# Sequence mixer of a two-layer block: five halving levels and a block of four, a solve without masked copies, the gate product ahead of the core steps

## The chip, the core and the metric

One core of one Trainium2 chip. The metric is the device time of one execution in microseconds (us). The kernel before takes 1794.52 us, the median of 3 runs (1789.35 to 1795.16). TensorE (PE) multiplies matrices, VectorE (DVE) and ScalarE (ACT) work on elements, GpSimd (POOL) here fills and copies a little, and SyncE (SP) issues the loads.

## The reference

256 tokens of width 1024 pass two layers, each a gated feed-forward, a hybrid mixer and a second feed-forward, and then a second block with retention and dilated attention. The change concerns the mixers alone:

```python
proj = h @ w_in            # split into hg_q, hg_f, hg_i, hg_g, gd_q, gd_k, gd_v, gd_z, gd_b, gd_a, rg_x, rg_gate
f = lbf + (1 - lbf) * sigmoid(hg_f)
o_hg = hgrn2_chunked(silu(hg_q) * 64**-0.5, 1 - f, hg_i, log(f))     # forgetting attention
o_hg = head_rmsnorm(o_hg) * silu(hg_g)
qkv = silu(causal_depthwise_conv(concat(gd_q, gd_k, gd_v)))
o_gd = gated_delta_chunked(l2norm(cq) * 128**-0.5, l2norm(ck), cv, g, beta)   # a triangular solve per chunk
o_gd = head_rmsnorm(o_gd) * silu(gd_z)
o_rg = rg_lru(...) * gelu(rg_gate)
return concat(o_hg, o_gd, o_rg) @ w_out
```

The forgetting attention scores a query at t and a key at s by the sum over channels of q k exp(cum_t - cum_s), where cum is the running sum of log f. The delta rule solves (I + L) u = rhs with L strictly lower triangular.

## The kernel before, in words

All wide matmuls are fp32 products in three passes over a high and a low half of each operand. A chunk of weights (128x1024) is loaded, cast on ScalarE to its high half wh (L92) and subtracted on VectorE to its low half wl (L93), in one of three buffers. TensorE then runs the passes, with 256 columns (L184 to L186) or up to 512 (L140 to L142), into one of four PSUM accumulators called mm.

A mixer's steps are written in the order of MIX_ORDER (L490). A scheduler places the recorded instructions on the engines by estimated times, and each engine then runs its own list in order. So small work of one step stands between the wide matmuls of others. The steps that matter here are these, for 256 tokens as two halves of 128.

- `delta_k` makes the matrices LT (line L676 writes them, scr in the trace) for the two halves and the cross part.
- `delta_solve` (twice per mixer) inverts I + L for four heads at once. It masks LT into a 32-block diagonal LTb (L715), a 32-off-diagonal LT32 (L720) and a 64-off-diagonal part (L721), on VectorE, with the sign changed. Then it doubles the block size: per size 2, 4, 8, 16 two groups of four small matmuls (L711, into the PSUM tile sv; x8 in the trace), a masked copy (L728), a transpose (L731) and a copy on ScalarE (L732). The sizes 32 and 64 follow with copies (L739, L750, L756) and scalings (L745, L746) on VectorE and copies and scalings on ScalarE (L743, L749, L759). Each group waits for the elements of the one before.
- `hg_scores` builds the scores S of the forgetting attention in seven halving levels (b = 64 to 1). A level takes differences to a reference position (L901, L902), an exponential on ScalarE, products with k and q (L904, L910), four matmuls and a masked copy into S (L917). The diagonal (t = s) is one product of q and k (L873), four small matmuls (hd, L878; x8 in the trace) and a masked copy of the identity.
- `gates` spreads the decay over 128 columns (gb, L601) before a matmul; `hg_vg` scales the values (L857).
- `delta_core` (twice) makes the delta rule's outputs (Zp, LZ, og). The z projection follows it in MIX_ORDER: 260 columns by `gemm_tok`, then `z_gate`, a tanh on ScalarE (L572) and a product on VectorE (L573). `delta_out` multiplies output, norm and gate (L792) and transposes the result (yT), and `project` runs 96 matmuls of 512 columns with w_out, first for the channels of the other two branches.

## Time and profile before

| | before |
|---|---|
| median of 3 runs | 1794.52 us |
| the profiled execution | 1796.44 us, its span 1794.7 us |
| granted TensorE clock, mean | 0.981 |
| mixer 0, mixer 1 | about 205 to 388 us, 765 to 945 us of the span |
| busy, TensorE, VectorE, ScalarE | 1734.5, 1207.1, 892.3 us |
| share of TensorE in the chain that ended last | 90% |

A wait in brackets behind an instruction is idle time of its engine just before it, with the instruction that ended it. PEclk is the clock granted to TensorE as a share of 2.4 GHz, 0.5 being 1.2 GHz. Only in the mixers, of all of the kernel, does the change alter a line.

### The profile page before, as it was taken

To read this page: it belongs to the slowest core of one execution; us is meant where nothing else is said; L and a number is where in the kernel's file an instruction comes from. 1 tells how busy PE (TensorE), PEld (TensorE's weight loads), DVE (VectorE), ACT (ScalarE), POOL (GpSimd) and SP (SyncE) were. 2 spreads that over 40 slices of the span, in tenths; PEclk is the share of its full clock that TensorE was granted. 3 is DMA by queue.
4 is the path that set the end of the run, shared out by engine and by line. 5 is a ranking of instruction groups with operands and counts; after the bars stand their busy time and mean duration, and the time that the engine had idled before them with its cause. 6 is when DMAs were issued, how large, how long until landed. Compare 5 with 4: busy or idle time off the path is not lost.

```text
span 1794.7 us, 28677 instructions
## 1 busy us (share of the span) xinstructions
PE 1734.5 (97%) x11296; PEld 1568.8 (87%) x11296; DVE 1207.1 (67%) x2181; ACT 892.3 (50%) x1352; POOL 13.4 (1%) x40
## 2 busy tenths in 40 slices
PE   8999989989999999989889999999999999999996
PEld 8997989879998999889879998888888788799885
DVE  6666689866655665589967665745666666766566
ACT  5444574444444444466345444555454544455454
POOL 0000000000000000000000000000000000000000
PEclk9999999899999999999989999999999999999998
DMA  6546542235565555543315556555443456645561
GB/s 233 186 153 220 163 135 84 94 104 185 176 197 189 183 188 181 186 151 118 127 47 177 187 169 199 185 176 173 133 130 124 146 176 211 200 155 198 194 229 53
DMA packets 91654, 292.38 MB, mean 163 GB/s; under 512 B 11008, under 2 KB 23808, under 8 KB 91520
## 3 DMA queue, kind: packets, MB, share of 16 engines
q1 hardware_dynamic: 91376, 290.45, 49.4%
q8 instruction: 88, 1.44, 0.3%
q14 instruction: 46, 0.38, 0.1%
q10 hardware_dynamic: 144, 0.11, 0.0%
HBM read 289.47 MB, written 1.05 MB: 162 GB/s over the span
## 4 chain that ended last, share of the span: by engine, by line
PE 90%; DVE 6%; ACT 2%; issue 1%; DMA 1%; SPq 0%; DVEq 0%; ACTq 0%
PE mm L185 13%; PE mm L186 13%; PE mm L184 13%; PE mm L140 13%; PE mm L141 13%; PE mm L142 13%; PE sv L711 2%; DVE wl L93 1%; ACT wh L92 1%; PE pv L1234 1%; PE dS L658 1%; PE dsc L1202 1%; PE hS L915 1%; PE dsc L1201 0%; DVE cv L630 0%
## 5 line engine op out<-in xcount | busy, mean ns | idle before, releaser
L93 DVE TENSOR_TENSOR wl<-raw,wh 128x1024 fp32r<-128x1024 f32 (+2 forms) x544 | 639.8, 1177 | 462.8 <-ACT wh L92 461.4
L92 ACT CAST wh<-raw 128x1024 fp32r<-128x1024 f32 (+2 forms) x544 | 549.3, 1011 | 652.1 <-PE mm L185 281.0
L184 PE MATMUL mm<-xTh,wh 128*128 128x256 f32 x2112 | 595.6, 284 | 13.1 <-DVE xp L622 10.0
L185 PE MATMUL mm<-xTl,wh 128*128 128x256 f32 x2112 | 598.0, 284 | 2.2 <-DVE xTl L197 2.1
L186 PE MATMUL mm<-xTh,wl 128*128 128x256 f32 x2112 | 595.2, 283 | 0.8 <-DVE wl L93 0.7
L184 PEld LDWEIGHTS mm<-xTh,wh 128*128 128x128 f32 x2112 | 401.4, 191 | 17.9 <-ACT th L572 10.4
L185 PEld LDWEIGHTS mm<-xTl,wh 128*128 128x128 f32 x2112 | 402.5, 191 | 4.7 <-DVE xTl L197 3.7
L186 PEld LDWEIGHTS mm<-xTh,wl 128*128 128x128 f32 x2112 | 403.0, 191 | 2.8 <-DVE wl L93 1.3
L141 PE MATMUL mm<-wl,hT 128*128 128x512 f32 x608 | 241.4, 398 | 2.4 <-DVE wl L93 2.4
L142 PE MATMUL mm<-wh,hT 128*128 128x512 f32 x608 | 238.8, 394 | 0.0
L140 PE MATMUL mm<-wh,hT 128*128 128x512 f32 x608 | 219.3, 397 | 4.8 <-DVE scr L573 4.8
L141 PE MATMUL mm<-wl,xTh 128*128 128x512 f32 (+1 forms) x440 | 169.3, 386 | 0.0
L142 PE MATMUL mm<-wh,xTl 128*128 128x512 f32 (+1 forms) x440 | 166.2, 380 | 0.0
L140 PE MATMUL mm<-wh,xTh 128*128 128x512 f32 (+1 forms) x440 | 160.2, 384 | 2.5 <-ACT xTh L196 2.5
L140 PEld LDWEIGHTS mm<-wh,hT 128*128 128x128 f32 x608 | 114.9, 190 | 30.2 <-DVE scr L573 5.2
L141 PEld LDWEIGHTS mm<-wl,hT 128*128 128x128 f32 x608 | 115.4, 190 | 28.3 <-DVE wl L93 3.9
L142 PEld LDWEIGHTS mm<-wh,hT 128*128 128x128 f32 x608 | 115.2, 189 | 24.7 <-DVE hT L197 0.2
L140 PEld LDWEIGHTS mm<-wh,xTh 128*128 128x128 f32 x440 | 82.0, 188 | 19.0 <-ACT xTh L196 2.9
L142 PEld LDWEIGHTS mm<-wh,xTl 128*128 128x128 f32 x440 | 83.0, 189 | 16.6 <-issue 2.0
L141 PEld LDWEIGHTS mm<-wl,xTh 128*128 128x128 f32 x440 | 82.9, 188 | 16.2 <-issue 1.9
L196 ACT ACTIVATE xTh<-xtr,colp 128x256 fp32r<-128x256 f32 (+1 forms) x72 | 28.9, 453 | 12.4 <-DVE xTl L197 12.3
L711 PE MATMUL sv<-hS,LTm 128*128 128x32 f32 x192 | 27.5, 293 | 7.3 <-ACT hS L732 4.3
...
## 6 DMA issues: line engine op xcount, KB each, us to landing
...
```

The source lines that it names most:

```text
L92: nc.scalar.copy(h, raw)
L93: nc.vector.tensor_tensor(l, raw, h.bitcast(F32), op=ALU.subtract)
L140: nc.tensor.matmul(o, xh[:, kt, tok], wh[:, k], start=a and k == 0, stop=False)
L141: nc.tensor.matmul(o, xh[:, kt, tok], wl[:, k], start=False, stop=False)
L142: nc.tensor.matmul(o, xl[:, kt, tok], wh[:, k], start=False, stop=z and k == m - 1)
L184: nc.tensor.matmul(o, wh[:, k, cs], xh[:, kt], start=a, stop=False)
L185: nc.tensor.matmul(o, wh[:, k, cs], xl[:, kt], start=False, stop=False)
L186: nc.tensor.matmul(o, wl[:, k, cs], xh[:, kt], start=False, stop=z)
L196: nc.scalar.activation(h, src, AF.Copy, scale=scale)
L658: nc.tensor.matmul(ps[:, h], k[:, h, sb * P:(sb + 1) * P], src[:, h, tb * P:(tb + 1) * P], start=True, stop=True)
L711: nc.tensor.matmul(o[:, h], lhsT[:, h], rhs[:, h], start=True, stop=True)
L915: nc.tensor.matmul(ps[:, i], B[:, j, t * P:(t + 1) * P], Q[:, i].rearrange("p h t -> p (h t)"), start=True, stop=True)
```

## The change

`hg_scores` stops halving at b = 4. What is left within blocks of four tokens (on and below the diagonal) is done at once: with differences to the second token of each block, one exponential for q and one of the opposite sign for k, two products, eight matmuls of half the rows, and two masked copies with the constant g4. The diagonal step (hd) goes. Within a level the key product covers only the even halves and is written in place. For b = 64 and 32 the scores go into S by plain copies on ScalarE in place of a masked copy.

`delta_solve` no longer masks. POOL fills LTb and LT32 with zeros and ScalarE copies the blocks into them with the sign changed; the product for size 64 uses the first 64 rows alone. Copies and scalings of the sizes 32 and 64 go from VectorE to ScalarE.

`gates` hands the matmul a broadcast view in place of gb. `hg_vg` scales the values on ScalarE. `delta_out` multiplies output and gate first, then the norm, 512 columns at a time. In MIX_ORDER z stands before the cores.

```diff
-LEVELS = (64, 32, 16, 8, 4, 2, 1)
+LEVELS = (64, 32, 16, 8, 4)
...
+    out["g4"] = ((t // 4 == s // 4) & (t >= s)).T * 1.0
...
-MIX_ORDER = "... dv1 q dv0 dq core0 core1 z dout out".split()
+MIX_ORDER = "... dv1 q dv0 dq z core0 core1 dout out".split()
...
-            gb = v2(c.w2("gb")[:, :4 * P], 4)
-            nc.vector.tensor_copy(gb, bc(g[:, t].unsqueeze(2), [P, 4, P]))
...
-                nc.tensor.matmul(ps[:, h], gb[:, h], c.K["triu"], start=True, stop=True)
+                nc.tensor.matmul(ps[:, h], bc(g[:, t, h:h + 1], [P, P]), c.K["triu"], start=True, stop=True)
...
+        def neg(o, i):
+            nc.scalar.activation(o, i, AF.Copy, scale=-1.0)
...
-        nc.vector.tensor_tensor(LTb, LT, h4(K["bd"]), op=ALU.mult)
+        nc.gpsimd.memset(LTb, 0.0)
+        nc.gpsimd.memset(LT32, 0.0)
+        for q in range(4):
+            neg(LTb[qd(q), :, qd(q)], LT[qd(q), :, qd(q)])
...
-        nc.vector.tensor_tensor(LT32, LT, h4(K["mt32"]), op=ALU.mult)
-        nc.vector.tensor_tensor(LT, LT, h4(K["mt64"]), op=ALU.mult)
+        for q in (0, 2):
+            neg(LT32[qd(q), :, qd(q + 1)], LT[qd(q), :, qd(q + 1)])
...
-            nc.vector.tensor_copy(PF[qd(q), :, qd(q - 1)], ps[qd(q)])
+            nc.scalar.copy(PF[qd(q), :, qd(q - 1)], ps[qd(q)])
...
-            nc.vector.tensor_scalar(T64[:, :, qd(q)], Tc, K["q2"][:, q:q + 1], None, op0=ALU.mult)
-            nc.vector.tensor_scalar(TT64[:, :, qd(q)], TTc, K["q2"][:, q:q + 1], None, op0=ALU.mult)
+            nc.scalar.activation(T64[:, :, qd(q)], Tc, AF.Copy, scale=K["q2"][:, q:q + 1])
+            nc.scalar.activation(TT64[:, :, qd(q)], TTc, AF.Copy, scale=K["q2"][:, q:q + 1])
...
-        nc.vector.tensor_copy(TT64[qd(2), :, 32:64], pq[qd(2)])
+        nc.scalar.copy(TT64[qd(2), :, 32:64], pq[qd(2)])
...
-        mm4(ps, LT, T64)
+        mm4(ps, LT[0:64], T64[0:64])
...
-        nc.vector.tensor_copy(PF[64:, :, 0:64], ps[64:])
+        neg(PF[64:, :, 0:64], ps[64:])
...
-            for h in range(4):
-                nc.vector.scalar_tensor_tensor(yt[:, h], self.og[t][:, h], self.gs[t][:, h:h + 1], sz[:, h],
-                                               op0=ALU.mult, op1=ALU.mult)
+            nc.vector.tensor_tensor(yt, self.og[t], sz, op=ALU.mult)
+            nc.vector.tensor_tensor(yt, yt, bc(self.gs[t].unsqueeze(2), [P, 4, P]), op=ALU.mult)
...
-            nc.vector.tensor_scalar(self.hv[:, t], ps[t][:, :256], self.r[:, t:t + 1], 1.0 / 16, op0=ALU.mult, op1=ALU.mult)
+            nc.scalar.activation(self.hv[:, t], ps[t][:, :256], AF.Copy, scale=self.r16[:, t:t + 1])
...
-        qk = v2(c.w2("hqk"), 2)
-        nc.vector.tensor_tensor(qk, q, k, op=ALU.mult)
...
-            nc.vector.tensor_tensor(B, A, k, op=ALU.mult)
+            nc.vector.tensor_tensor(Av[:, :, 0], Av[:, :, 0], f(k)[:, :, 0], op=ALU.mult)
...
+            if b >= 32:
+                for i in range(n):
+                    sp = slice(2 * b * i, 2 * b * i + b)
+                    nc.scalar.copy(S[sp, :, 2 * b * i + b:2 * b * (i + 1)], ps[sp, :, b * i:b * (i + 1)])
...
+        nc.vector.tensor_tensor(f4(A), f4(cum), bc(f4(cum)[:, :, 1:2], [P, P, 4]), op=ALU.subtract)
+        nc.scalar.activation(C, A, AF.Exp)
+        nc.scalar.activation(B, A, AF.Exp, scale=-1.0)
+        nc.vector.tensor_tensor(B, B, k, op=ALU.mult)
+        nc.vector.tensor_tensor(Q, C, q, op=ALU.mult)
+        for par in range(2):
+            pp = slice(par * 64, par * 64 + 64)
+            ps = v2(c.x_tile("hS"), 4)
+            for i in range(4):
+                tt = slice((i % 2) * P, (i % 2 + 1) * P)
+                nc.tensor.matmul(ps[:, i], B[pp, i // 2, tt], Q[pp, i // 2, tt], start=True, stop=True)
+            nc.vector.copy_predicated(S.rearrange("p (i h) t -> p i h t", h=2)[:, :, par],
+                                      bc(c.K["g4"].bitcast(I32).unsqueeze(1), [P, 4, P]), ps)
```

The new kernel's lines have moved: L715 to L720 are its L720 to L725, L739 its L743, L711 its L709, L813 its L816. What the scheduler makes of it is a new order on every engine. Three places follow. A number behind a name is that of a buffer.

VectorE where the solve starts in mixer 0, from the scan over log f on. Before:

```order
L846 SCALAR_TENSOR_TENSOR scr_2230<-seg,lf_2997 128x512
L676 TENSOR_TENSOR scr_2224<-dS_2745,scr_2227 128x512
L715 TENSOR_TENSOR LTm_2772<-scr_2224,ctab 128x512
L720 TENSOR_TENSOR LTm_2773<-scr_2224,ctab 128x512
L676 TENSOR_TENSOR scr_2224<-dS_2755,scr_2227 128x512
L718 COPY_PREDICATED hS_2229<-ctab,LTm_2772 32x128 x4
L721 TENSOR_TENSOR scr_2224<-scr_2224,ctab 128x512
L676 TENSOR_TENSOR scr_2224<-dS_2765,scr_2227 128x512
L851 SCALAR_TENSOR_TENSOR scr_2230<-th_3002,qx_3001 128x512
L715 TENSOR_TENSOR LTm_3364<-scr_2224,ctab 128x512
L720 TENSOR_TENSOR LTm_3365<-scr_2224,ctab 128x512
L719 STREAM_TRANSPOSE hS_2229<-hS_2229 128x128
```

Now:

```order
L849 SCALAR_TENSOR_TENSOR scr_2232<-seg,lf_3000 128x512
L93 TENSOR_TENSOR wl_3201<-raw_3198,wh_3200 128x1024
L854 SCALAR_TENSOR_TENSOR scr_2232<-th_3005,qx_3004 128x512
L722 COPY_PREDICATED hS_2231<-ctab,LTm_2770 32x128 x3
L878 TENSOR_TENSOR hA_3094<-scr_2232 128x2x128
L722 COPY_PREDICATED hS_2231<-ctab,LTm_2770 32x128
L722 COPY_PREDICATED hS_2231<-ctab,LTm_3348 32x128 x4
L723 STREAM_TRANSPOSE hS_2231<-hS_2231 128x128
L93 TENSOR_TENSOR wl_3231<-raw_3228,wh_3230 128x1024
L723 STREAM_TRANSPOSE hS_2231<-hS_2231 128x128
```

The three masked copies of each half (L715, L720, L721) are gone, and the low half of the next weight chunk (L93) now stands ahead of the copies into hS and their transposes (L723, before L719).

ScalarE at the end of the two solves in mixer 1 (sv_8536 and sv_9133 before, sv_8519 and sv_9102 now, are their PSUM tiles). Before:

```order
L633 ACTIVATE th_9127<-cv_9104 128x512
L92 CAST wh_9697<-raw_9695 128x1024
L633 ACTIVATE th_9130<-cv_9104 128x512
L936 ACTIVATE sqh_9228<-oh_9229 128x256
L936 ACTIVATE sqh_9228<-oh_9235 128x256
L749 COPY scr_7990<-sv_8536 32x4x32
L732 COPY hS_7994<-sv_9133 128x128
L743 ACTIVATE scr_7990<-hS_7994,ctab 128x4x32 x4
L749 COPY scr_7990<-sv_8536 32x4x32
L749 COPY scr_7990<-sv_9133 32x4x32 x2
```

Now:

```order
L736 COPY hS_7981<-sv_8519 128x128
L749 ACTIVATE scr_7978<-hS_7981,ctab 128x4x32 x2
L736 COPY hS_7981<-sv_9102 128x128
L749 ACTIVATE scr_7978<-hS_7981,ctab 128x4x32 x2
L747 ACTIVATE scr_7977<-hS_7981,ctab 128x4x32 x4
L750 ACTIVATE scr_7978<-hS_7981,ctab 128x4x32 x2
L747 ACTIVATE scr_7977<-hS_7981,ctab 128x4x32 x4
L750 ACTIVATE scr_7978<-hS_7981,ctab 128x4x32 x2
L743 COPY LTm_8520<-sv_8519 32x4x32 x2
L743 COPY LTm_9103<-sv_9102 32x4x32 x2
```

Sixteen scalings (L749, L747, L750) stand in a row, but for one L736, ahead of the four copies L743, which stood on VectorE before (L739).

TensorE at the end of the z projection (xTh, xTl) in mixer 1, up to project's first matmuls (hT). Before:

```order
L141 MATMUL mm_9552<-wl_9610,xTh_7913 128x260
L142 MATMUL mm_9552<-wh_9609,xTl_7914 128x260
L711 MATMUL sv_8536<-hS_7994,LTm_8537 128x32 x4
L711 MATMUL sv_9133<-hS_7994,scr_7990 128x32 x4
L711 MATMUL sv_9133<-hS_7994,LTm_9135 128x32 x4
L711 MATMUL sv_9133<-hS_7994,LTm_9134 128x32 x4
L711 MATMUL sv_8536<-scr_7991,scr_7989 128x64 x4
L813 MATMUL yT_9265<-ident,yth_9263 128x128 x2
L813 MATMUL yT_9272<-ident,yth_9270 128x128 x2
L140 MATMUL mm_9655<-wh_9661,hT_7987 128x512
L141 MATMUL mm_9655<-wl_9662,hT_7987 128x512
```

Now:

```order
L142 MATMUL mm_9454<-wh_9511,xTl_7899 128x260
L709 MATMUL sv_8519<-hS_7981,scr_7977 128x32 x4
L140 MATMUL mm_9454<-wh_9511,xTh_7898 128x260
L141 MATMUL mm_9454<-wl_9512,xTh_7898 128x260
L142 MATMUL mm_9454<-wh_9511,xTl_7899 128x260
L709 MATMUL sv_9102<-hS_7981,scr_7977 128x32 x4
L709 MATMUL sv_8519<-hS_7981,LTm_8521 128x32 x4
L709 MATMUL sv_9102<-hS_7981,LTm_9104 128x32 x4
L816 MATMUL yT_9239<-ident,yth_9237 128x128 x2
L816 MATMUL yT_9246<-ident,yth_9244 128x128 x2
L140 MATMUL mm_9625<-wh_9631,hT_7974 128x512
L141 MATMUL mm_9625<-wl_9632,hT_7974 128x512
```

Five groups of the solve stood back to back, and now three do; the rest stand further on among project's matmuls. In both versions the z matmuls stand ahead of the core steps. Between them and the last output matmul (og) 24 of project's 96 matmuls stood in each mixer, and now 48 do.

## Rows read from the trace of the kernel before

**Rows 1.** the page, part 1: busy us (share) xinstructions
```profile
PE 1734.5 (97%) x11296; PEld 1568.8 (87%) x11296; DVE 1207.1 (67%) x2181; ACT 892.3 (50%) x1352; POOL 13.4 (1%) x40
```
**Rows 2.** 10-us stretches, mixer 0: length; busy by engine; PEclk; DMA share; GB/s
```profile
270.00:280.00 10.00, 7.51 (x37) 6.92 (x36) 9.90 (x19) 4.48 (x7) 0.00 (x0) 0.70 0.33 111
...
300.00:310.00 10.00, 10.00 (x91) 10.00 (x89) 9.88 (x21) 2.79 (x6) 0.21 (x2) 1.00 0.10 27
...
330.00:340.00 10.00, 7.14 (x39) 6.90 (x37) 9.38 (x28) 3.10 (x8) 0.94 (x4) 0.60 0.32 106
340.00:350.00 10.00, 10.00 (x46) 8.87 (x47) 9.75 (x24) 4.92 (x12) 0.95 (x1) 0.72 0.00 0
...
sum 160.00, PE 144.40 PEld 134.31 DVE 138.14 ACT 84.69 POOL 4.97; mean PE 9.03 PEld 8.39 DVE 8.63 ACT 5.29 POOL 0.31
```
**Rows 3.** the same stretches in mixer 1
```profile
890.00:900.00 10.00, 7.32 (x30) 6.76 (x31) 9.26 (x31) 3.37 (x11) 0.65 (x3) 0.50 0.49 171
...
920.00:930.00 10.00, 6.73 (x32) 5.61 (x33) 7.38 (x34) 2.54 (x5) 0.00 (x0) 0.83 0.01 2
...
sum 160.00, PE 143.32 PEld 132.74 DVE 139.51 ACT 86.10 POOL 2.89; mean PE 8.96 PEld 8.30 DVE 8.72 ACT 5.38 POOL 0.18
```
**Rows 4.** waits of PE, 205 to 390 us: total, times, longest us
```profile
PE mm L184 <- DVE xp L622: 5.0, 1, 5.0
PE mm L140 <- DVE scr L573: 2.4, 1, 2.4
PE sv L711 <- DVE hgm L941: 2.0, 1, 2.0
...
PE sv L711 <- ACT hS L732: 0.9, 1, 0.9
```
**Rows 5.** waits of PE, 765 to 950 us
```profile
PE sv L711 <- ACT hS L732: 3.4, 1, 3.4
...
PE sv L711 <- DVE LTm L739: 1.4, 1, 1.4
...
PE mm L186 <- DVE wl L93: 0.7, 1, 0.7
```
**Rows 6.** DVE groups by form, 200 to 400 us: busy, mean ns | idle before
```profile
L917 DVE COPY_PREDICATED hS<-ctab,hS 128x512 f32<-128x512 int32 x7 | 6.2, 881 | 0.0
...
L720 DVE TENSOR_TENSOR LTm<-scr,ctab 128x512 f32<-128x512 f32 x2 | 1.4, 685 | 0.0
...
L739 DVE COPY LTm<-sv 32x128 f32<-32x128 f32 x4 | 1.2, 290 | 0.2
...
L745 DVE TENSOR_SCALAR scr<-hS,ctab 128x128 f32<-128x128 f32 x4 | 1.1, 403 | 0.0
```
**Rows 7.** groups on ACT by form, same stretch
```profile
L743 ACT ACTIVATE scr<-hS,ctab 128x128 f32<-128x128 f32 x8 | 2.6, 390 | 0.1
L749 ACT COPY scr<-sv 32x128 f32<-32x128 f32 x4 | 1.0, 252 | 5.3 <-DVE scr L748 5.3
```
**Rows 8.** timeline, 264 to 281 us: start, length, engine, instruction, [idle before <-releaser]
```profile
271.23 0.39 PE L184 MATMUL mm<-xTh,wh 128*128 128x256 f32 x1 [0.91 <-ACT wh L92]
...
273.56 1.58 PE L711 MATMUL sv<-hS,LTm 128*128 128x32 f32 x8 [1.59 <-DVE hS L719]
273.79 2.35 DVE L93 TENSOR_TENSOR wl<-raw,wh 128x1024 fp32r<-128x1024 f32 x2
```
**Rows 9.** timeline, 328 to 347 us
```profile
330.14 0.97 PE L711 MATMUL sv<-hS,LTm 128*128 128x32 f32 x8
...
331.10 1.22 DVE L93 TENSOR_TENSOR wl<-raw,wh 128x1024 fp32r<-128x1024 f32 x1
...
333.12 1.92 PE L711 MATMUL sv<-hS,scr 128*128 128x32 f32 x8 [2.00 <-DVE hgm L941]
```
**Rows 10.** timeline, 355 to 377 us
```profile
363.16 0.17 DVE L212 TENSOR_SCALAR rsa<-rsw 128x4 f32<-128x4 f32 x1
...
367.85 0.50 PE L140 MATMUL mm<-wh,hT 128*128 128x512 f32 x1 [2.39 <-DVE scr L573]
```

More of the change, by code (lines that the diff above doesn't have):

```diff
@@ L348, in consts_np @@
     own = lambda a: np.stack([a[r, 32 * (r // 32):32 * (r // 32) + 32] for r in range(P)])
-    for b in LEVELS:
+    for b in (16, 8, 4, 2, 1):
         m = (t // (2 * b) == s // (2 * b)) & ((t // b) % 2 == 1) & ((s // b) % 2 == 0)
         odd = np.nonzero((i // b) % 2)[0]
-        out[f"mc{b}"] = m[odd].T * 1.0
-        if b in (32, 64):
-            out[f"mt{b}"] = m.T * -1.0
-        elif b > 1:
+        if b in LEVELS:
+            out[f"mc{b}"] = m[odd].T * 1.0
+        if b > 1:
             out[f"m{b}"] = m * 1.0
@@ L358, in consts_np @@
             out["mto1"] = own(m.T * 1.0)
-    out["bd"] = (t // 32 == s // 32) * -1.0
+    out["g4"] = ((t // 4 == s // 4) & (t >= s)).T * 1.0
     out["io"] = own(np.eye(P))
@@ L362, in consts_np @@
     out["q2"] = (i[:, None] // 32 % 2 == np.arange(2)) * 1.0
-    out["hind"] = np.stack([(i < 64) * 1.0, (i >= 64) * 1.0], 1)
     layout, o = {}, 0
@@ L486, in v2 @@
     return ap.rearrange("p (a b) -> p a b", a=a)
-MIX_ORDER = "rg ba k gates dk solve0 hg vg hgs v solve1 hgo both dv1 q dv0 dq core0 core1 z dout out".split()
+MIX_ORDER = "rg ba k gates dk solve0 hg vg hgs v solve1 hgo both dv1 q dv0 dq z core0 core1 dout out".split()
 class Mixer:
@@ L500, in __init__ @@
         c.nc.vector.tensor_scalar(self.rh, self.r, 0.5, None, op0=ALU.mult)
+        self.r16 = c.small.tile([P, 2], F32, tag="r16", name=c.nm("r16"))
+        c.nc.vector.tensor_scalar(self.r16, self.r, 1.0 / 16, None, op0=ALU.mult)
         self.y = c.hT_tile(0)
@@ L865, in hg_scores @@
         q, k, cum = self.q, self.k, self.cum
-        fl = lambda a: a.rearrange("p a b -> p (a b)")
         S = self.S
+        qd = lambda x: slice(32 * x, 32 * x + 32)
         nc.gpsimd.memset(S, 0.0)
@@ L870, in hg_scores @@
             nc.gpsimd.memset(z, 0.0)
-        qk = v2(c.w2("hqk"), 2)
-        nc.vector.tensor_tensor(qk, q, k, op=ALU.mult)
-        pd = c.x_tile("hd")
-        for j in range(2):
-            for t in range(2):
-                i = 2 * j + t
-                nc.tensor.matmul(pd[:, 2 * i:2 * i + 2], qk[:, j, t * P:(t + 1) * P], c.K["hind"], start=True, stop=True)
-        nc.vector.copy_predicated(S, bc(c.K["ident"].bitcast(I32).unsqueeze(1), [P, 8, P]),
-                                  bc(pd[:, :8].unsqueeze(2), [P, 8, P]))
         A, B = v2(c.w2("hA"), 2), v2(c.w2("hB"), 2)
@@ L910, in hg_scores @@
                 nc.vector.tensor_tensor(o, g(A)[pp, :, :, 1], g(q)[pp, :, :, 1], op=ALU.mult)
-            ps = c.x_tile("hS").rearrange("p (i t) -> p i t", i=4)
-            for j in range(2):
-                for t in range(2):
-                    i = 2 * j + t
-                    nc.tensor.matmul(ps[:, i], B[:, j, t * P:(t + 1) * P], Q[:, i].rearrange("p h t -> p (h t)"),
-                                     start=True, stop=True)
-            nc.vector.copy_predicated(
-                S.rearrange("p i (n two b) -> p i n two b", two=2, b=b)[:, :, :, 1],
-                bc(c.K[f"mc{b}"].bitcast(I32).rearrange("p (n b) -> p n b", b=b).unsqueeze(1), [P, 8, n, b]),
-                ps.rearrange("p i (h n b) -> p (i h) n b", h=2, b=b))
+            ps = c.x_tile("hS").rearrange("p (i t) -> p i t", i=8)
@@ new lines, in hg_scores @@
+            for i in range(4):
+                nc.tensor.matmul(ps[:, 2 * i:2 * i + 2].rearrange("p h t -> p (h t)"), A[:, i // 2, (i % 2) * P:(i % 2 + 1) * P],
+                                 Q[:, i].rearrange("p h t -> p (h t)"), start=True, stop=True)
+            if b >= 32:
+                for i in range(n):
+                    sp = slice(2 * b * i, 2 * b * i + b)
+                    nc.scalar.copy(S[sp, :, 2 * b * i + b:2 * b * (i + 1)], ps[sp, :, b * i:b * (i + 1)])
+            else:
+                nc.vector.copy_predicated(
+                    S.rearrange("p i (n two b) -> p i n two b", two=2, b=b)[:, :, :, 1],
+                    bc(c.K[f"mc{b}"].bitcast(I32).rearrange("p (n b) -> p n b", b=b).unsqueeze(1), [P, 8, n, b]),
+                    ps.rearrange("p i (n b) -> p i n b", b=b))
```

6 lines of the change are left out of this document (5 added, 1 removed).

## Prediction

> **What bounds the kernel now.** I read the page first. TensorE is busy for 97% of the span and VectorE for 67% [rows 1], so an instruction taken off VectorE is worth something only where TensorE waits for it, or runs at its lower clock because it had waited. Next I cut the two mixers into 10 us stretches, as the change touches nothing outside them. Of 160 us TensorE is busy 144.4 in mixer 0 and 143.3 in mixer 1 [rows 2, 3]: it idles 15.6 and 16.7 us. From 300 to 310 us it is full at full clock while VectorE is full too [rows 2]. There the forgetting attention costs nothing that can be saved, because wide projection matmuls cover it. The loss sits in three places.
>
> Place one is the start of the solve in mixer 0. Stretch 270 to 280 has TensorE busy 7.51 at a granted clock of 0.70 [rows 2]: it idles 2.5 and loses some 7.5 x 0.3 = 2.2 by the clock. Its two waits are 0.91 for a weight cast and 1.59 for a transpose on VectorE, and the low halves of the next weights (L93) stand on VectorE behind that transpose [rows 8]. Place two is the end of the solve. In mixer 0 a group of eight small matmuls (L711) takes 0.97 at 330.14; behind a wait of 2.00 the next takes 1.92, the lower clock of 1.2 instead of 2.4 GHz [rows 9]. The stretches 330 to 350 have clocks of 0.60 and 0.72 [rows 2]. In mixer 1 the waits are 3.4 and 1.4 [rows 5] and stretch 890 to 900 runs at 0.50 [rows 3]. Place three follows the last core step: project's second column half waits 2.39 for the z gate's product [rows 10], in both mixers. One large wait is no part of this: 5.0 us for the padded convolution input [rows 4] stands before all that is changed, and stays.
>
> **VectorE in sum.** Per mixer the change takes away six masked copies (0.69 each by L720 [rows 6], 4.1 us), four predicated copies (0.88 by L917, 3.5), and, by the same forms and those near them, the diagonal copy and its product (2), two levels' differences and products (4.7), half of five wide products (1.3), copies and scalings in two solves (5.3), gate copies and value scalings (1.8). It adds three wide operations and two predicated copies (3.8). That is about 19 us less per mixer, 38 in all. ScalarE takes some 11 us more per mixer (12 negations and some 14 copies, 0.25 by L749 and the wide ones up to 0.6, and 8 scalings near 0.39 [rows 7]). POOL gets four more fills per mixer; it is 1% busy [rows 1]. No DMA is added; the constant table is smaller and is loaded once. So the 38 us are no gain by themselves; I price them place by place.
>
> **Matmuls removed.** Eight small ones for the diagonal, as the trace counts them, go in each mixer, at 0.12 (eight take 0.97 [rows 9]): -0.95 each, as TensorE is full there. Bounds: 0 to -0.95. The levels' matmuls keep their number: two levels go, and the blocks of four bring as many. The 64-row product in the solve streams the same columns: nothing.
>
> **Place one.** In the new order L93 stands ahead of the predicated copies, and the masked copies are twelve negations on ScalarE. If both waits and the slow clock go, mixer 0 gains 2.5 + 2.2 = 4.7; if ScalarE's negations are as late as VectorE's copies were, nothing. I take -3.5, nearer the gain, because the weights no longer queue behind the masks. In mixer 1 the counterpart is the wait of 0.7 for L93 [rows 5]: -0.6.
>
> **From 280 to 330.** Freed VectorE time is worth 0, the cover being the projections; a new order can add a wait. Its size is taken from the one short wait of that kind, 0.7 [rows 5]: +0.7 per mixer, bounds 0 and +2.0 (the wait of [rows 9]).
>
> **Place two.** What decides is how many small groups stand back to back. In mixer 1 five did: waits of 4.8, and five groups at half clock, 0.95 lost each, 9.5 in all. In the new order three do, the other groups having z or project matmuls between them, as project's first half no longer ends with 24 matmuls but with 48. I take one wait of 2.0 and three slow groups, 4.85: -4.7. In mixer 0 five groups also ran slow behind waits of 2.0 and 0.9 [rows 4], 7.6 in all; the new order has two pairs apart, but they stand earlier, with less filler ahead, so I keep one wait of 2.0 and nearly four slow groups, 5.6: -2.0. The copies that go to ScalarE cost the chain no more each: 0.290 for a 32x128 copy on VectorE [rows 6], 0.252 on ScalarE [rows 7]; a scaling 0.403 against 0.390. Bounds: +5.7 per mixer (third rival) to a full recovery, -8.5 (second).
>
> On the last point the Trainium skill speaks against the change: "ScalarE: Activation LUTs", section "Rules for kernel authors", says to multiply and add on VectorE rather than ScalarE, VectorE being up to about three times as fast per element in bf16. The rows disagree for these fp32 tiles, which are small. By that ratio, as an estimate from the page, sixteen chain copies at 0.6 more each would take back 9 us, and the sum would be near zero. What a loaded ScalarE would do here, by rows alone, is the third rival.
>
> **Place three.** The z product is moved ahead of the cores, so the wait of 2.39 goes. The z matmuls already stood ahead of the cores, so what moves is the product, the release of two accumulators and 24 matmuls of project (5.5 us). These no longer cover the end: after the last output matmul come some eleven small steps of 0.2 (0.17 and its gap [rows 10]), a product of 0.69 and a split of about the same. I put 3.5 in place of 2.4: +1.1 per mixer, bounds 0 and +3. In mixer 1 the following stretch ran at 0.83 [rows 3], 6.7 x 0.17 = 1.1; with a shorter slow spell before it I take -1.0, bounds 0 and -1.1.
>
> **Sum.** Mixer 0: -0.95 -3.5 +0.7 -2.0 +1.1 = -4.65. Mixer 1: -0.95 -0.6 +0.7 -4.7 +1.1 -1.0 = -5.45. Together -10.1 on the profiled 1796.4, which gives 1786.3. That run stood 1.9 above the median of 1794.5, so against the median I forecast **1784**. The bounds that lie near give 4 to 18 us of gain, 1776 to 1791.
>
> **Rivals.** Full recovery: with VectorE lighter and filler between the groups, the tail's waits go and the clock stays up. Mixer 0 then gains the lost 8.5 of stretches 330 to 350 instead of 2.0 (2.9 idle, 2.9 and 2.8 by the clock [rows 2]), mixer 1 all 9.5 instead of 4.7: 11.3 more, **1773**. For it: VectorE is 94% to 98% busy in those stretches. Against it: the solve is a serial chain across three engines.
>
> Idle gain: TensorE is the bound, and the freed time on VectorE ends in waits for other things. Only the removed matmuls (-1.9), place one (-3.5) and the stalls and lost cover (+3.6) count, near -2: **1793**. For it: in 300 to 310 TensorE is full. Against it: the waits named above end on VectorE work that is removed or moved.
>
> ScalarE becomes the queue, which is slower than before: in mixer 1 the copy that the solve's next product needs (L743 of the new kernel) stands behind sixteen scalings, at 0.32 each (eight take 2.6 [rows 7]) 5.1 us, where four stood ahead of the copies on ScalarE, 1.3; that is 3.8 more in the chain, and two more groups at half clock, 1.9. So the tail gains nothing and loses 5.7 in each mixer: -10.1 + 6.7 + 11.4 = +8.0, **1802**. It decides when the filler between two groups, a few matmuls of 0.11, is shorter than the queue on ScalarE. For it: 11 us more work and one in-order queue. Against it: ScalarE is busy 3.1 of 10 us from 330 to 340 [rows 2], so that most of it finds room.
>
> That the z move changes nothing can't be excluded either: place three then stays as it was, which takes the +2.2 out of the sum, 1782, inside the forecast's range.
>
> **Chances.** Forecast 0.52, full recovery 0.18, idle gain 0.18, ScalarE queue 0.12. A measurement of this kernel can tell about 0.3%, 5.4 us, from no change. Faster by more: 0.46 of the forecast, all of the recovery and 0.02 of the idle case, 0.66. Within: 0.06 of the forecast, 0.14 of the idle case and 0.02 of the last, 0.22. Slower: 0.12. The range is 1771 to 1798; about half of the recovery case lies below it and most of the ScalarE case above, together under 0.2.
>
> **What would show it.** Right: VectorE's busy time lower by 30 to 40 us and ScalarE's higher by about 20; no wait on the z product; in 270 to 280 of mixer 0 a clock near 1.0; in mixer 1 three small groups in a row near half clock instead of five; waits of 2 to 4 us behind the last output matmul. Wrong: a wait over 2 us on ScalarE's new copies or negations (then the ScalarE case), or TensorE's idle in the mixers unchanged at 32 us (the idle case), or clocks of 1.0 through the tails (full recovery).

## The result and the profile after

The changed kernel takes 1806.62 us (median of 6 runs, 1801.12 to 1810.56), the kernel before 1795.55 beside it (1789.35 to 1797.5). The ratio is **1.0062**, with a 95% interval of 1.0046 to 1.0078. It is slower by 11 us, where 1784 was forecast and 1771 to 1798 was the range. The profiled execution took 1805.69, its span 1803.8, at a mean granted clock of 0.976.

The page of the kernel after, parts 1 and 4, against [rows 1]:
```profile
PE 1739.8 (96%) x11280; PEld 1570.3 (87%) x11280; DVE 1174.3 (65%) x2101; ACT 912.0 (51%) x1418; POOL 18.6 (1%) x48
...
PE 89%; DVE 5%; ACT 4%; DMA 1%; issue 1%; SPq 0%; DVEq 0%; ACTq 0%
```
VectorE lost 32.8 us of work and ScalarE took on 19.7. TensorE issues 16 matmuls fewer and is yet busy for 5.3 us longer. Work that is less and lasts longer is work at a lower clock.

The two mixers of the kernel after, each from the transposes that open it to those that open the part behind it (length; busy us of PE, PEld, DVE, ACT, POOL; PEclk; DMA share; GB/s), then stretches of mixer 1 and of mixer 0:
```profile
205.35:387.62 182.27, 166.01 (x1173) 154.71 (x1172) 139.12 (x318) 106.02 (x209) 7.83 (x19) 0.93 0.32 104
766.91:957.39 190.48, 174.22 (x1173) 161.77 (x1171) 139.91 (x320) 105.40 (x210) 3.81 (x11) 0.89 0.32 108
880.00:890.00 10.00, 10.00 (x63) 10.00 (x62) 4.08 (x9) 2.10 (x5) 1.06 (x2) 0.65 0.32 107
890.00:900.00 10.00, 10.00 (x41) 9.32 (x42) 5.89 (x17) 8.33 (x26) 1.16 (x4) 0.50 0.42 140
900.00:910.00 10.00, 8.12 (x52) 6.84 (x50) 9.75 (x21) 7.71 (x20) 0.00 (x0) 0.99 0.29 112
910.00:920.00 10.00, 10.00 (x46) 9.56 (x46) 1.97 (x5) 2.35 (x7) 0.00 (x0) 0.52 0.16 52
...
270.00:280.00 10.00, 7.09 (x56) 6.40 (x55) 9.08 (x19) 9.71 (x23) 1.24 (x1) 1.00 0.27 93
330.00:340.00 10.00, 8.28 (x54) 7.21 (x53) 9.81 (x21) 9.54 (x28) 2.46 (x4) 1.00 0.48 157
340.00:350.00 10.00, 9.58 (x44) 9.16 (x44) 3.52 (x7) 4.27 (x13) 0.52 (x1) 0.52 0.16 54
```
The same cut gives 181.30 and 180.38 for the two mixers before. So mixer 0 is 1.0 longer and **mixer 1 is 10.1 longer**: nearly all of the loss lies there. From 880 to 900 and from 910 to 920 TensorE is busy for all of the 30 us and yet gets little done, at clocks of 0.50 to 0.65. In 1 us steps the half clock covers 42 us of mixer 1, where it covered 24 before; by PE busy x (1 - PEclk) that costs 19.5 us instead of 9.3. TensorE's idle time there hardly changed, from 16.0 to 16.3.

The waits of TensorE in the kernel after, from 205 to 390 us (total, times, longest us), against [rows 4]:
```profile
PE mm L184 <- DVE xp L620: 5.6, 1, 5.6
PE yT L816 <- DVE hms L807: 2.7, 1, 2.7
PE mm L184 <- ACT wh L92: 1.7, 1, 1.7
PE sv L709 <- ACT LTm L712: 1.2, 1, 1.2
...
PE mm L140 <- ACT hT L196: 0.8, 1, 0.8
```
The wait of 2.4 for the z product is gone, and so is the one of 2.0 in the solve. In their place stand 2.7 for the output's transpose behind VectorE, 1.7 for a weight cast and 1.2 for the new negations (L712). Mixer 1 has the 2.7 too.

### The profile page after: what moved, and what is told of

Read it like the earlier page. It is cut to its first block, busy times and chain, and to the rows that moved or that the text cites. A ratio compares the mean times of both kernels' runs of the same rounds, so it can differ in the third digit from the quotient of the medians.

```text
span 1803.8 us, 28654 instructions
## 1 busy us (share of the span) xinstructions
PE 1739.8 (96%) x11280; PEld 1570.3 (87%) x11280; DVE 1174.3 (65%) x2101; ACT 912.0 (51%) x1418; POOL 18.6 (1%) x48
## 3 DMA queue, kind: packets, MB, share of 16 engines
HBM read 289.21 MB, written 1.05 MB: 161 GB/s over the span
## 4 chain that ended last, share of the span: by engine, by line
PE 89%; DVE 5%; ACT 4%; DMA 1%; issue 1%; SPq 0%; DVEq 0%; ACTq 0%
PE mm L141 13%; PE mm L140 13%; PE mm L142 13%; PE mm L185 13%; PE mm L186 13%; PE mm L184 13%; PE sv L709 2%; DVE wl L93 1%; ACT wh L92 1%; PE dS L656 1%; PE pv L1249 1%; PE dsc L1217 1%; DMA raw<-in_weights 1%; DVE cv L628 1%; PE hS L909 1%
## 5 line engine op out<-in xcount | busy, mean ns | idle before, releaser
L93 DVE TENSOR_TENSOR wl<-raw,wh 128x1024 fp32r<-128x1024 f32 (+2 forms) x544 | 640.3, 1178 | 469.8 <-ACT wh L92 467.0
L184 PE MATMUL mm<-xTh,wh 128*128 128x256 f32 x2112 | 593.5, 283 | 17.1 <-DVE xp L620 10.4
L184 PEld LDWEIGHTS mm<-xTh,wh 128*128 128x128 f32 x2112 | 400.2, 190 | 22.5 <-ACT th L572 10.8
L197 DVE SCALAR_TENSOR_TENSOR xTl<-xtr,colp,xTh 128x256 fp32r<-128x256 f32 (+1 forms) x72 | 30.5, 450 | 3.7 <-ACT xTh L196 3.3
```

The lines of the kernel that those rows point to most:

```text
L93: nc.vector.tensor_tensor(l, raw, h.bitcast(F32), op=ALU.subtract)
L184: nc.tensor.matmul(o, wh[:, k, cs], xh[:, kt], start=a, stop=False)
L197: nc.vector.scalar_tensor_tensor(l, src, scale, h.bitcast(F32), op0=ALU.mult, op1=ALU.subtract)
```

## The experiments

The change has four parts that can be taken alone: **solve** (negations, copies and scalings on ScalarE, the 64-row product), **attention** (five levels and blocks of four), **z** (the entry of MIX_ORDER) and **product** (the output product in two wide operations on VectorE). A fifth, **small**, is the gate copy and the value scaling. In the table, "us" is the ratio's distance from 1 times 1795.5, and its interval reaches 3 to 5 us to either side. Most ratios agree with the distance of the two medians within about 1 us; in the small samples (4 runs each) the medians are -11.9 apart for e5, -7.8 for e12, -6.6 for e17 and +9.8 for e9, and for e18 they are -0.8 apart. The last columns are the lengths of the mixers in the profiled execution, which is one run and not a median: the executions of one kernel spread over 4 to 24 us, and the profiled ones of e1, e3, e13 and e15 lie 6.5 to 9 us below their medians. Part of that lies outside the mixers, where every kernel has the same lines and the profiled executions yet take from 1426.8 to 1436.1 us.

| run | parts in it | ratio, 95% | us | mixer 0 | mixer 1 |
|---|---|---|---|---|---|
| before | none | 1 | 0 | 181.3 | 180.4 |
| after | all | 1.0062 [1.0046, 1.0078] | +11.1 | 182.3 | 190.5 |
| e1 | z | 1.0000 [0.9982, 1.0019] | 0 | 181.6 | 179.6 |
| e2 | all but z | 1.0045 [1.0017, 1.0074] | +8.1 | 183.3 | 183.3 |
| e3 | all but solve | 1.0000 [0.9975, 1.0025] | 0 | 179.4 | 177.6 |
| e4 | all but attention | 1.0019 [1.0003, 1.0035] | +3.4 | 183.3 | 183.1 |
| e5 | solve | 0.9927 [0.9901, 0.9953] | -13.1 | 178.1 | 175.9 |
| e6 | all, scalings back | 1.0031 [1.0008, 1.0055] | +5.6 | 181.9 | 188.5 |
| e7 | all, copies back | 1.0074 [1.0052, 1.0097] | +13.3 | 187.6 | 190.2 |
| e8 | all, negations back | 1.0034 [1.0011, 1.0056] | +6.1 | 189.4 | 181.4 |
| e9 | all, wider matmuls | 1.0045 [1.0029, 1.0060] | +8.1 | 183.5 | 190.0 |
| e10 | solve, attention | 0.9981 [0.9963, 0.9999] | -3.4 | 176.8 | 183.6 |
| e11 | solve, z | 0.9963 [0.9946, 0.9980] | -6.6 | 179.2 | 177.6 |
| e12 | solve, wider matmuls | 0.9943 [0.9921, 0.9965] | -10.2 | 183.8 | 173.8 |
| e13 | z, product | 1.0042 [1.0017, 1.0066] | +7.5 | 184.8 | 181.2 |
| e14 | all but product | 1.0005 [0.9989, 1.0022] | +0.9 | 178.8 | 187.1 |
| e15 | attention | 0.9971 [0.9955, 0.9987] | -5.2 | 178.3 | 178.0 |
| e16 | as e14, other order | 0.9972 [0.9947, 0.9997] | -5.0 | 181.7 | 175.3 |
| e17 | all but z and product | 0.9942 [0.9921, 0.9962] | -10.4 | 186.6 | 174.3 |
| e18 | as e10, other order | 0.9983 [0.9958, 1.0007] | -3.1 | 176.5 | 184.2 |

### First: which part costs

The candidates were z, whose matmuls no longer cover the mixer's end, the solve on ScalarE, and the attention's new order.

**e1, z alone.**
```diff
-... dv1 q dv0 dq core0 core1 z dout out
+... dv1 q dv0 dq z core0 core1 dout out
```


> The kernel before with the z step alone moved ahead of the core steps. Clock theory (the loss of the change is TensorE at half clock in mixer 1, made by where small solve groups stand; the low-clock loss there went from 9.3 to 19.5 us while idle time stayed at 16): if the z move alone sets that order, this run is slower by 5 to 11 us than the kernel before, with low-clock time in mixer 1 well above 24 us. ScalarE-queue theory (copies moved to ScalarE lengthen the solve): no copy has moved, so within 3 us of before, or some 2 us better by the wait on the z product.


No change, 1.0000. Moving z neither costs nor gains: the mixers end 16.9 us behind the last output matmul instead of 22.5 and 23.9, but that matmul comes some 6 us later. The cover that z gave at the end is paid for where z now stands.

**e2, the full change without z.**
```diff
-... dv1 q dv0 dq z core0 core1 dout out
+... dv1 q dv0 dq core0 core1 z dout out
```


> The changed kernel with the z step back behind the core steps. Clock theory with the z move as cause: 1795 or less, as the low-clock loss in mixer 1 goes back to near 9 us and VectorE's relief remains. ScalarE-queue theory: stays near 1806, since all copies remain on ScalarE.


Still 8.1 us slower than before. With e1 that clears the z move of most of the loss.

**e3, the old solve in the changed kernel.**
```diff
-neg(LTb[qd(q), :, qd(q)], LT[qd(q), :, qd(q)])
+nc.vector.tensor_tensor(LTb, LT, h4(K["bd"]), op=ALU.mult)
...
```


> The changed kernel with the solve as before: masked copies, block copies and scalings on VectorE. ScalarE-queue theory: 1795 or less. Clock theory with the z move as cause: stays at 1803 or more. If both are wrong and the attention part matters, also near 1806.


As fast as before by the runs. Both mixers are shorter than before, but in an execution that was 7 us faster than this kernel's median.

**e4, the old attention in the changed kernel.**
```diff
-LEVELS = (64, 32, 16, 8, 4)
+LEVELS = (64, 32, 16, 8, 4, 2, 1)
...
```


> The changed kernel with the forgetting attention as before: seven levels and the diagonal step. If the earlier end of the attention is what bunches its output matmuls with the solve groups (small matmuls from 876 to 884 us with no idle, where the clock fell), this goes back to 1797 or less. Otherwise VectorE gets some 10 us per mixer more, where TensorE is full: the same 1806 within 3 us, plus 1.9 us for the diagonal matmuls.


3.4 us slower than before, about 8 faster than the change. Undoing either large part recovers most, so neither can be the cause by itself.

**e5, the solve alone** in the kernel before.
```diff
-nc.vector.tensor_tensor(LTb, LT, h4(K["bd"]), op=ALU.mult)
+neg(LTb[qd(q), :, qd(q)], LT[qd(q), :, qd(q)])
...
```


> The kernel before with the solve's part alone (zero fills on POOL, negated copies, block copies and scalings on ScalarE). If the moved solve is the whole cause: 6 to 11 us slower than before. If it costs only together with the shorter attention or the z move, which change what fills TensorE beside it: within 3 us of before.


The fastest of all: 1785.23 us, **0.9927**. Its two mixers by the same cut as above:
```profile
203.20:381.20 178.00, 163.42 (x1180) 152.74 (x1179) 147.37 (x336) 104.66 (x204) 8.40 (x19) 0.94 0.32 107
760.50:936.40 175.90, 163.27 (x1181) 152.22 (x1180) 147.47 (x338) 103.94 (x205) 3.11 (x11) 0.95 0.34 117
```
ScalarE is about as busy here as in the changed kernel (104.66 and 103.94, against 106.02 and 105.40), and the mixers are 3.2 and 4.5 shorter than before. That is 7.8 of the 13.9 us between the two profiled executions; the other 6.1 lie outside the mixers, where no line differs, so the 13.1 may be too high.

### Second: is it the queue on ScalarE?

The theory is the prediction's third rival: copies on ScalarE that the solve waits for stand behind other work. If so, giving that work back to VectorE recovers the loss.

**e6, scalings back on VectorE; e7, copies back; e8, negations back.**
```diff
-nc.scalar.activation(T64[:, :, qd(q)], Tc, AF.Copy, scale=K["q2"][:, q:q + 1])
+nc.vector.tensor_scalar(T64[:, :, qd(q)], Tc, K["q2"][:, q:q + 1], None, op0=ALU.mult)
```


> The changed kernel with the eight scalings L749 and L750 of each mixer back on VectorE. Scalings theory: in mixer 1 the copy L743 that the solve's next group needs ran at 897.76, behind sixteen scalings from 892.52 on, while its input was there some 3 us earlier; then this run goes back to 1799 or less. Copies theory (each chain copy on ScalarE waits for casts and convolutions): stays at 1804 or more.


```diff
-nc.scalar.copy(PF[qd(q), :, qd(q - 1)], ps[qd(q)])
+nc.vector.tensor_copy(PF[qd(q), :, qd(q - 1)], ps[qd(q)])
```


> The changed kernel with the block copies L743, L754 and the negated copy of size 64 back on VectorE, the scalings left on ScalarE. Copies theory: 1799 or less, and the waits of TensorE on L754 and L712 (1.7, 0.9 and 1.2 us) are gone. Scalings theory: the copies no longer stand behind the scalings in ScalarE's queue, so it goes back too; it stays at 1804 or more only if the start of the solve (negated copies) is the cause.


```diff
-neg(LTb[qd(q), :, qd(q)], LT[qd(q), :, qd(q)])
+nc.vector.tensor_scalar(LTb[qd(q), :, qd(q)], LT[qd(q), :, qd(q)], -1.0, None, op0=ALU.mult)
```


> The changed kernel with the twelve negated copies per mixer at the start of the solve on VectorE. Start theory (ScalarE is 9.7 of 10 us busy from 830 to 840, and TensorE idles 3.4 there): 1800 or less. Scalings or copies theory: stays at 1804 or more.


None comes back to the kernel before: +5.6, +13.3 and +6.1. The queue does stand there, in the timeline of ScalarE in the kernel after, mixer 1 (start, length, instruction, [idle before <-releaser]):
```profile
894.13 1.27 ACT L747 ACTIVATE scr<-hS,ctab 128x128 f32<-128x128 f32 x4
...
895.88 1.27 ACT L747 ACTIVATE scr<-hS,ctab 128x128 f32<-128x128 f32 x4
...
897.76 1.07 ACT L743 COPY LTm<-sv 32x128 f32<-32x128 f32 x4
```
The copy L743 waits for the scalings, as that rival said. But e6 takes half of the sixteen scalings out and mixer 1 still takes 188.5, and e5 has all of them on ScalarE and is the fastest. So the rival came close in the number, 1802, and falls as a cause by itself. Inside the full change ScalarE's part of the solve does count: e3, which takes all of it back together with the masks, recovers the whole 11 us, and e6 and e8 some 5 each, with intervals that overlap that of the changed kernel. In e8 the long mixer is mixer 0 (189.4): the loss changed places instead of going.

### Third: small matmuls at half clock?

In mixer 1 the clock falls at 883.1 while TensorE is fed without a pause. The timeline of PE in the kernel after:
```profile
882.21 1.05 PE L709 MATMUL sv<-hS,LTm 128*128 128x32 f32 x8
883.08 0.67 PE L949 MATMUL oh<-scr,hS 128*128 128x64 f32 x2
...
883.93 0.57 PE L141 MATMUL mm<-wl,xTh 128*128 128x260 f32 x1
...
885.38 1.75 PE L709 MATMUL sv<-hS,LTm 128*128 128x32 f32 x8
```
Eight solve matmuls take 1.05, then 1.75, with nothing but matmuls between. The question is whether the clock falls here with these narrow matmuls (32 columns in L709, 64 in L949), and whether the mixer is longer because of it.

**e9, wider matmuls in the changed kernel; e12, in e5.** Three of four heads compute 64 columns in the solve and 128 in the attention's output, of which the surplus is never read.
```diff
+w = 64 if h < 3 else 32
+nc.tensor.matmul(o[:, h, :w], lhsT[:, h], f(rhs)[:, 32 * h:32 * h + w], start=True, stop=True)
```


> The changed kernel with wider small matmuls: in the solve's groups three of four heads take 64 columns in place of 32 (the rest lands in columns that nobody reads), in the attention's output 128 in place of 64. Numbers of instructions, the chain and the order in mixer 0 are the same; a group of 64 columns took 1.0 to 1.1 us at full clock where one of 32 took 0.97. Clock theory (the clock falls and stays low because TensorE streams few columns there): low-clock time falls from 42 us in mixer 1 and 23 in mixer 0 to 45 or less in sum, and the run is 5 us or more below the changed kernel. Chain theory (the clock follows the waits): same low-clock time, and 0 to 3 us slower.

> The fastest so far, the solve's part alone, with the wider small matmuls of the run on columns. Clock theory: its low-clock time of 22 and 19 us falls by half, 1778 to 1783. Chain theory: 1785 to 1788.


Mixer 1 of e9, stretches and one wait:
```profile
880.00:890.00 10.00, 10.00 (x89) 10.00 (x89) 6.21 (x13) 2.76 (x6) 1.05 (x2) 1.00 0.31 107
890.00:900.00 10.00, 8.73 (x63) 7.67 (x61) 7.19 (x21) 9.66 (x30) 1.15 (x4) 1.00 0.53 192
900.00:910.00 10.00, 5.88 (x27) 4.80 (x25) 8.61 (x18) 6.92 (x18) 0.00 (x0) 0.81 0.26 84
910.00:920.00 10.00, 10.00 (x46) 9.69 (x45) 1.46 (x4) 1.27 (x4) 0.00 (x0) 0.50 0.07 28
...
PE ssl L647 <- ACT sq L643: 4.1, 1, 4.1
```
The clock of 880 to 900 is 1.00 instead of 0.65 and 0.50, and mixer 1 is 190.0 instead of 190.5. The clock gave back 5.7 us by the same sum as above. Idle time took 3.7 of it: 16.3 became 20.0, with a wait of 4.1 for the squares that follow the q convolution. The steps show where the lead went. The matmuls of these squares (ssl) start 138.1 us behind the mixer's start instead of 142.4, so up to there 4.3 us are won; at the end of the solve 1.3 are left, and at the end of the mixer 0.5. In between the clock is at half again (0.52 and 0.50 from 910 to 920). So the first half-clock stretch is **not the whole cause**: without it the mixer is as long. That the chain across VectorE and ScalarE sets the end there is only argued, for up to the squares that chain came forward too. In e12 mixer 0 grew and mixer 1 shrank, -10.2 in all against e5's -13.1; its scheduled order of matmuls moved too, so it decides nothing.

### Fourth: pairs

The theory now: solve and attention, good alone, collide, as each frees VectorE and brings the other's steps forward.

**e10, solve and attention; e11, solve and z.** The hunks of both parts, no others.
```diff
+LEVELS = (64, 32, 16, 8, 4)
+neg(LTb[qd(q), :, qd(q)], LT[qd(q), :, qd(q)])
...
```


> The kernel before with the solve's part and the five-level attention, nothing else. The solve alone gave -12 us against before, all four parts +9. If the attention is the part that does not go with it, this is at 1795 or more. If not, VectorE has yet less to do: 1786 or less.


```diff
+neg(LTb[qd(q), :, qd(q)], LT[qd(q), :, qd(q)])
+... dq z core0 core1 dout out
...
```


> The kernel before with the solve's part and the z step ahead of the core steps. If the z move is the part that does not go with the solve, 1793 or more; if not, near 1785, perhaps 2 us less by the wait on the z product.


**e15, attention alone.**
```diff
-LEVELS = (64, 32, 16, 8, 4, 2, 1)
+LEVELS = (64, 32, 16, 8, 4)
...
```


> The kernel before with the five-level attention alone. Collision theory: the shorter attention lets the value convolution start 18 us earlier (86 to 89 us after the mixer's start in every version with it, 104 to 109 in every version without it), and its work on VectorE and ScalarE stands ahead of the solve's serial steps, so that the solve ends at 148 us or later against 143 to 148 before: within 4 us of before, though VectorE has about 10 us less to do per mixer. Relief theory: VectorE's relief shortens the tail as in the run with the solve alone, 1790 or less.


Alone the attention gains 5.2 and the solve 13.1; together they gain 3.4, not 18.3. Mixer 0 of e10 keeps the gain (176.8), mixer 1 loses it (183.6, of which 17.1 go by the clock). Solve and z give -6.6, not -13.1.

**e13, z and product; e14, all but product.**
```diff
-for h in range(4):
-    nc.vector.scalar_tensor_tensor(yt[:, h], self.og[t][:, h], self.gs[t][:, h:h + 1], sz[:, h], ...)
+nc.vector.tensor_tensor(yt, self.og[t], sz, op=ALU.mult)
+nc.vector.tensor_tensor(yt, yt, bc(self.gs[t].unsqueeze(2), [P, 4, P]), op=ALU.mult)
```


> The kernel before with the z move and the new output product (two products of 512 columns in place of four of 128). With the z move alone the mixer ended 16.9 us after its last output matmul, in the changed kernel 20.1 and 20.4. Product theory (on VectorE's in-order queue the second half's first product, which waits for its output, stands ahead of the first half's second product, which is ready): 3 to 3.6 us slower per mixer than the z move alone, so 1803 to 1806 and 20 us behind the last output matmul. Rival (the longer end has to do with the solve or attention): 1798 within 2, and 17 us.

> The changed kernel with the output product as before (four products of 128 columns). Product theory: 7 us faster than the changed kernel, 1799 to 1801, with 17 us behind the last output matmul; what remains above the solve's part alone (1785) is the end of the solve, at 148 us or later after the mixer's start. Rival: 1805 or more.


The product is a cause, shown from both sides: e13 is 7.5 above e1, the changed kernel about 10 above e14. The timeline of the changed kernel at the end of mixer 1 shows how:
```profile
935.93 0.68 DVE L795 TENSOR_TENSOR yt<-scr,scr 128x512 f32<-128x512 f32 x1
...
937.04 0.58 ACT L787 COPY scr<-og 128x512 f32<-128x512 f32 x1 [1.92 <-PE og L785]
...
937.66 0.69 DVE L795 TENSOR_TENSOR yt<-scr,scr 128x512 f32<-128x512 f32 x1 [1.05 <-ACT scr L787]
938.32 0.69 DVE L806 TENSOR_REDUCE hms<-sqo 128x4 f32<-128x512 f32 x1
938.92 0.68 DVE L796 TENSOR_TENSOR yt<-yt,hrs 128x512 f32<-128x512 f32 x1
...
939.75 0.63 PE L816 MATMUL yT<-ident,yt 128*128 128x128 f32 x4 [2.75 <-DVE hms L807]
```
and that of e14, with the old product:
```profile
932.89 0.17 DVE L223 SCALAR_TENSOR_TENSOR hrs<-rsa,rsy 128x4 f32<-128x4 f32 x1
...
933.09 1.14 DVE L798 SCALAR_TENSOR_TENSOR yt<-scr,hrs,scr 128x128 f32<-128x128 f32 x4
...
933.88 0.73 PE L819 MATMUL yT<-ident,yt 128*128 128x128 f32 x4
```
The old product of the first half is four instructions with nothing between them. They start at 933.09, as soon as the scale `hrs` is there, and its transpose on TensorE follows without a wait. The new one is split. Its first operation is done at 936.61; its second (L796, 938.92) comes behind the second half's first operation, which idles VectorE for 1.05 until ScalarE's copy, and behind that half's reduction. VectorE works in order, so a product whose operands are ready stands behind one whose operands are not, and TensorE waits 2.75. The stretch from the last output matmul to the end of mixer 1 shows the price, first in the changed kernel, then in e14:
```profile
937.01:957.39 20.38, 16.05 (x69) 12.40 (x69) 12.26 (x25) 8.80 (x15) 0.00 (x0) 0.92 0.16 55
934.05:950.92 16.87, 14.71 (x68) 10.98 (x67) 11.62 (x27) 8.67 (x15) 0.00 (x0) 1.00 0.19 66
```
It is 3.5 longer: TensorE idles 4.3 instead of 2.2, and behind the wait it works at a clock of 0.92 instead of 1.00, which costs the rest. Mixer 0 shows the same (20.1 against 16.9), and so do e13 and e1 (21.4 and 20.4 against 16.9 twice). In sum this is 6.7 us for the changed kernel and 8.0 for e13, most of what the runs show for the one and all of it for the other.

### Fifth: what else decides between the mixers

e14 still has a long mixer 1:
```profile
205.70:384.50 178.80, 165.42 (x1172) 153.83 (x1171) 139.01 (x322) 105.79 (x209) 7.84 (x19) 0.94 0.32 106
763.80:950.90 187.10, 173.15 (x1172) 160.83 (x1171) 139.62 (x324) 105.38 (x210) 3.80 (x11) 0.90 0.32 110
```
**e16, solve1 ahead of v in e14; e18, the same in e10; e17, e14 without z.**
```diff
-... hg vg hgs v solve1 hgo both ...
+... hg vg hgs solve1 v hgo both ...
```


> The changed kernel with the old output product and with the value projection and convolution written behind the second solve. Collision theory: the solve's last group ends earlier than in the run with the old product alone, and the time is 4 us or more below it, 1795 or less. Rival (where the solve stands among the convolution does not matter): within 2 us of the run with the old product.

> Solve and attention alone (1793), with the second solve written ahead of the value projection. That order took 6 us off the changed kernel with the old product, 12 off in mixer 1. If the loss of solve and attention together is an accident of the order in mixer 1, this is 1787 or less; if it belongs to the two parts, 1793 within 2.


```diff
-... dv1 q dv0 dq z core0 core1 dout out
+... dv1 q dv0 dq core0 core1 z dout out
```


> The changed kernel without the z move and with the old output product: solve, attention, the gate copies left out and the value scaling on ScalarE. Solve and attention without the last two gave 1793, the same with the new product 1806. If the product costs its 7 to 9 us without the z move too, this is 1797 to 1799. If the gate and value edits cost nothing, 1793 within 2. If they cost what is missing, 1800 or more.


The edit of e16 was to bring the value convolution behind the second solve. It still starts 90 us after the mixer's start (88 in e14), so the run doesn't test that. Its mixer 1 came down to 175.3, its mixer 0 rose to 181.7. The same edit did nothing in e10 (e18: 184.2 in mixer 1). In e17 mixer 1 is good and mixer 0 long:
```profile
206.00:392.60 186.60, 172.56 (x1173) 161.82 (x1172) 138.84 (x322) 106.01 (x209) 7.87 (x19) 0.89 0.31 102
771.90:946.20 174.30, 163.49 (x1173) 152.69 (x1172) 139.36 (x324) 105.42 (x210) 3.00 (x11) 0.94 0.36 118
```
The two mixers of e17 hold the same matmuls, and their TensorE work differs by 9 us, all of it clock (0.89 and 0.94). The same holds for the two of e14, the other way round. Of the eleven kernels with solve and attention together, nine have a mixer of 183.5 or more, e2 has two of 183.3, and only e16 stays below 182. Of the nine without both, e4 and e13 with the product and e12 pass 183; the others stay at 181.6 or below. In eight of those nine kernels the longest mixer loses 17.1 to 21.4 us by the clock, by the sum used above, and no other mixer of any kernel loses more than 13.8. The exception is e9, whose long mixer loses 13.8 and idles 20.0.

The long form is no accident of one execution. The changed kernel and e14 differ only in the output product, and their last output matmuls end 162.2 and 161.9 us into mixer 0, 170.1 and 170.2 us into mixer 1, with the same solve groups at half clock on the way. So the form goes with the order of the instructions.

## Why the prediction was wrong

**Right.** VectorE's work went down by 33 us (30 to 40 forecast), ScalarE's up by 20 (about 20). The wait on the z product is gone. Stretch 270 to 280 runs at 1.00, where it ran at 0.70 [rows 2]. Behind the last output matmul of each mixer TensorE waits 2.7 + 0.8 = 3.5, the figure put in place of 2.4; that it is met is luck, as place three shows.

**Place one** was half right. The clock came back, but new waits took the place of the old: 1.7 for the weight cast and 1.2 for L712. TensorE's busy time in that stretch is 7.09, less than the 7.51 before [rows 2]. With the product's cost at the end, mixer 0 is 1.0 longer, where -4.65 was forecast.

**Place two is the step that failed first.** The prediction counted the groups of small matmuls that stand back to back, took five slow ones down to three in mixer 1 and booked -4.7. Already the count before was misread. Of the five groups in mixer 1 of the kernel before (each is eight matmuls in the trace) the first two ran at full clock, and three at half:
```profile
885.32 0.97 PE L711 MATMUL sv<-hS,LTm 128*128 128x32 f32 x8
886.13 1.06 PE L711 MATMUL sv<-hS,scr 128*128 128x32 f32 x8
...
890.60 1.92 PE L711 MATMUL sv<-hS,LTm 128*128 128x32 f32 x8 [3.41 <-ACT hS L732]
...
893.95 1.89 PE L711 MATMUL sv<-hS,LTm 128*128 128x32 f32 x8 [1.43 <-DVE LTm L739]
...
895.65 1.95 PE L711 MATMUL sv<-scr,scr 128*128 128x64 f32 x8
```
In the kernel after eight ran at half clock (the line of sixteen is two of them):
```profile
885.38 1.75 PE L709 MATMUL sv<-hS,LTm 128*128 128x32 f32 x8
...
888.82 1.75 PE L709 MATMUL sv<-hS,scr 128*128 128x32 f32 x8
...
891.17 1.75 PE L709 MATMUL sv<-hS,scr 128*128 128x32 f32 x8
892.74 3.60 PE L709 MATMUL sv<-hS,LTm 128*128 128x32 f32 x16
...
911.30 1.97 PE L709 MATMUL sv<-scr,scr 64*128 64x64 f32 x8
...
914.21 1.81 PE L709 MATMUL sv<-scr,LTm 128*128 128x64 f32 x8
...
918.05 1.80 PE L709 MATMUL sv<-scr,LTm 128*128 128x64 f32 x8
```
So the term was a loss of five groups and not a gain of two, and the wide matmuls beside them were slow too: two stretches near half clock of 17 and 14 us, in a mixer that is 10.1 longer. (In mixer 0 the term came out better than booked: five slow groups became two, where nearly four were kept.) Two premises failed. The first is that the clock falls only behind a wait: at 883.1 it fell with TensorE busy throughout. The second is that the slow groups are the price, one by one: e9 removed one of the two stretches and the mixer kept its length.

**Place three** had the right wait, the wrong owner and too small a price. The z move alone is worth 0.0 (e1): the last output matmul comes 6 us later and the end behind it is 6 us shorter. The 2.7 belongs to the split output product, which the prediction had only as less work on VectorE and as one step of 0.69. It booked +1.1 per mixer here; the product costs 7.5 us in the kernel, 3.2 to 4.5 per mixer behind the last output matmul. This is the second step that failed.

**The sum.** Alone, the parts measure -13.1 (solve), -5.2 (attention), 0 (z) and +7.5 (product, on z): -10.8, close to the -10.1 forecast, and by luck. The whole is +11.1. So 22 us are interplay, and a sum of places has no term for it. The mixers of the profiled executions alone say nearly the same: -7.8, -5.4, -0.6 and +4.9, together -8.9, against +11.1 for the whole. Of the pairs measured, solve with attention loses 15 by the runs (12 by the mixers) and solve with z 6.5 (3). That these come to 21.5 is not to be read as a full account: z on top of e17 costs 11 (5 by the mixers), and e17, which has the small part on top of e10, is 7 faster than it by the ratios but only 2 by the medians.

**The rivals.** The ScalarE queue, at 1802, came nearest to the time. As a cause by itself e5 takes it away, and its sign, a wait over 2 us on a new ScalarE copy, is not in the changed kernel, whose longest is 1.7 (L754, mixer 1). It shows up only in kernels that keep the old attention (2.2 each in e4, e5, e11 and e12), and three of these four are faster than the kernel before. What is left of it is that inside the full change the work given back helps. The sign set for the idle gain, TensorE's idle in the mixers unchanged at 32 us, did come (31.1 before, 32.6 after, by the cut of the table), but not its time of 1793: the loss is in the clock, which that rival left out. The prediction also weighed a rule of the Trainium skill, "ScalarE: Activation LUTs", section "Rules for kernel authors", which wants multiplications on VectorE. No run shows VectorE three times as fast on these small fp32 tiles: 0.290 against 0.252 us and 0.403 against 0.390 [rows 6, 7]. That the solve gains 13 us by itself on ScalarE is no test of the rule, since it also drops three wide masked copies per half. Inside the full change the rule's direction fits in part: giving the scalings back to VectorE helped by 5.5 (e6) and the negations by 5 (e8), at the edge of the intervals, and the copies not at all (e7).

**Open.** Which step makes one mixer fall into the long form once solve and attention are both in. That a small edit moves it from one mixer to the other (e8, e17) or takes it away (e16) is shown. That the two solves then run in step, or that the q convolution queues behind them on VectorE and ScalarE, was only argued.
